# Two weight loads of a feed-forward stage issued by GpSimd, out of the queue of x's loads and stores

## The chip, the cores and the metric

One core of a Trainium2 chip runs the kernel. The metric is the device time of one execution in microseconds. The engines are named as the profile names them: PE is TensorE (matmuls), PEld its weight loads, DVE is VectorE, ACT is ScalarE, POOL is GpSimd, SP is SyncE; SPq and POOLq are the issues of transfers on SP and POOL.

## What is computed

One step of a hybrid encoder layer for a prompt of 512 frames and a sample of 64: adaLN modulation, an input projection, sparse attention, a Mamba-2 scan, a gated merge, and a SwiGLU feed-forward, all in float32. The change lies where the merge's output projection ends and the feed-forward begins:

```python
mixed = (g_attn * (o_attn @ w_branch_attn) + g_ssm * (y @ w_branch_ssm)) @ w_out
x = x + gt1 * mixed
h2 = rms_normalize(x) * g_norm_ffn * (1.0 + sc2) + sh2
gate, up = jnp.split(h2 @ w_gate_up, 2, axis=-1)
x = x + gt2 * ((jax.nn.silu(gate) * up) @ w_down)
```

D_MODEL is 1024, the feed-forward is 2816 wide; `gt1`, `sc2`, `sh2` and `gt2` are pieces of the adaLN modulation `silu(c) @ w_ada`.

## The kernel before

The kernel is written against a planner (`Plan`). Each operation is recorded, and `order` plays all of them through a model of costs, queues and latencies, and so fixes in which order each engine issues its instructions; `emit` then writes them out. Every instruction therefore has the line of the helper, L533, in the profile, and groups are told apart by the names of tiles. Since the order of an engine is fixed, an instruction that waits holds up all behind it on that engine. `R.after(ops)` adds edges to the planner's model alone; it makes no semaphore.

The 576 frames are held transposed, channels on partitions, in two halves of 288 columns (`hf` 0 and 1). A float32 product is made of three float32r matmuls, with both operands split in a high and a low part: `wh`, `wl` for weights, `mh`, `ml` for the merged activations, `xh…`, `xl…` for the feed-forward's input. ScalarE rounds the high part, VectorE subtracts to get the low one.

The output projection makes eight blocks `a` of 128 channels (`pwo0` to `pwo7`), 24 matmuls for each half. Blocks 0 to 4 are done both halves together; of blocks 5, 6 and 7 the first half comes first, then the second. Two PSUM slots named `mm` serve blocks 0 to 6 in turn, so block 6 takes the slot of block 4; block 7 lies in `px` and `py`. After each block and half, `residual` runs: VectorE adds `gt1 * mixed` to x in two pieces (256 and 32 columns, prompt and sample), ScalarE squares the result (`sq`) and scales it into `y2` (256 and 32 columns), VectorE adds the squares up (`sqa`). x is loaded from `x_d` by SyncE, in four buffers (`x2`, bufs=4): when a block is done, its x is stored, and the x of four blocks later is loaded into the same buffer. When the squares of block 7 are in, six small matmuls (`px<-ones,sqa`) sum them, GpSimd takes the power -1/2, TensorE spreads it over the partitions, and VectorE and ScalarE make the feed-forward's operands `xhA`, `xlA`.

In the same stretch `ada_columns(10, ...)` works out a piece of the modulation: GpSimd issues eight loads of `w_ada`, 256 KB each, into two buffers named T1 and T2 in turn (the trace leaves numbers out: `T<-in_w_ada`); VectorE multiplies each into two accumulators (T3, T4), which frees the buffer for the next but one, and two groups of eight small matmuls (`px<-T,pick`) end it.

The feed-forward's weights come in 22 slices `f`. `load_f(f)` loads two tiles of 512 KB, rows of 512 bytes, 128 x 8 of them: `g` (rows for the gate, tag `raw`, two buffers that the output projection's weights use too) and `u` (for the up part, tag `rawu`, two buffers of its own). `g0`, `u0` stand for those of slice 0, and so on; the third use of a `rawu` buffer, u2 and u3, waits until u0 and u1 are used up. `prepare` makes one operand out of a quarter of such a pair. Operands 6 and 7 are the two quarters of u1; they have buffers of their own (`wx`), so they can be made before the products start. The slices 0 and 1 are done plainly, the others by Strassen's scheme with seven products; all of them are bound to a list, `steps`, and TensorE walks through it.

SyncE's one queue carries, in this stretch, the last weights of the output projection, the loads and stores of x, and all the feed-forward's weights.

Of the kernel before, what the change touches and what calls it, by code (L numbers as in the profile page):

```python
# [13 lines left out]
P = 128  # L14
# [9 lines left out]
DFF = 2816  # L24
# [516 lines left out]
def build(tc, I, O):  # L541
    R = Plan(tc)
    vec, act, pool, pe, sync = R.vec, R.act, R.pool, R.pe, R.sync
# [51 lines left out]
    def kview(src2d):  # L595
        return src2d.rearrange("(k p) n -> p k n", p=P)
# [209 lines left out]
    x_d = R.dram([P, 8, 2, TH], F32, name="x_d")  # L806
# [762 lines left out]
    xqh, xql = {}, {}  # L1569
    ffw = R.mkpool("ffw", reuse_waits="tile")  # L1570
    x2p = R.mkpool("x2", reuse_waits="tile")
    x2 = {}

    y2 = {(j, hf): x2p.tile([P, 2, TW], F32, name=f"y2{j}{hf}") for j in range(4) for hf in range(2)}
    sqa = [x2p.tile([P, TH], F32, name=f"sqa{hf}") for hf in range(2)]

    def load_x2(a):
        x2[a] = x2p.tile([P, 2, TH], F32, name=f"x2{a}", tag="x2", bufs=4)
        sync.dma_start(x2[a], x_d[:, a])

    for a in range(4):
        load_x2(a)
# [6 lines left out]
    def residual(a, ps, hf, last):  # L1589
        x = x2[a][:, hf]  # L1590
        for s, c0, n in SEG:
            vec.scalar_tensor_tensor(x[:, c0:c0 + n], ps[:, c0:c0 + n], gt1h[:, a, s:s + 1], x[:, c0:c0 + n], op0=OP.mult, op1=OP.add)
        if a == 0:
            act.activation(sqa[hf], x, AF.Square)
        else:
            sq = x2p.tile([P, TH], F32, name=f"sq2{a}{hf}", tag="sq2", bufs=2)
            act.activation(sq, x, AF.Square)
            vec.tensor_tensor(sqa[hf], sqa[hf], sq, OP.add)
        for s, c0, n in SEG:
            act.activation(y2[a // 2, hf][:, a % 2, c0:c0 + n], x[:, c0:c0 + n], AF.Copy, scale=A2[:, a, s:s + 1])  # L1600
        if hf == 1:
            sync.dma_start(x2_d[:, a], x2[a])
            if a + 4 < 8:
                load_x2(a + 4)
# [81 lines left out]
    w_gu = I["w_gate_up"][0]  # L1686
# [4 lines left out]
    def load_f(f):  # L1691
        g = wp.tile([P, 8, P], F32, name=f"rawg{f}", tag="raw", bufs=2)
        u = ffw.tile([P, 8, P], F32, name=f"rawu{f}", tag="rawu", bufs=2)
        sync.dma_start(g, kview(w_gu[:, P * f:P * f + P]))
        sync.dma_start(u, kview(w_gu[:, DFF + P * f:DFF + P * f + P]))
        rawf[f] = {"B11": g[:, 0:4], "B21": g[:, 4:8], "B12": u[:, 0:4], "B22": u[:, 4:8]}

    def weight_sum(f, q):
# [10 lines left out]
    def prepare():  # L1709
        j = made[0]  # L1710
        f, q = preps[j]
        pl, tag, bufs = (x2p, "wx", 2) if 6 <= j < NP0 else (wp, ("wh", "wl")[j % 2], NWH)
        wops[f, q] = t = pl.tile([P, 8, P], F32R, name=f"wf{j}", tag=tag, bufs=bufs)
        src = rawf[f][q] if q[0] == "B" else weight_sum(f, q)
        act.activation(t[:, 0:4], src, AF.Copy)
        vec.tensor_tensor(t[:, 4:8], src, t[:, 0:4].bitcast(F32), OP.subtract)
        left[f] -= 1
        if left[f] == 0 and f + 2 < NFT:
            load_f(f + 2)
        made[0] += 1  # L1720
# [90 lines left out]
    def free_after(j):  # L1811

        return -1 if j < NP0 else N0 // 2 + j - NP0 if j < NP0 + 6 else N0 + j - 6 - NP0

    load_f(0)
    load_f(1)
    for i, (f, w, x, b, starts, *p) in enumerate(steps):
        if i in LATE_OPERANDS:
# [275 lines left out]
```

## Time and profile before

| | us |
|---|---|
| runs of the kernel (three) | 1373.69, 1377.72, 1378.02 |
| their median | 1377.72 |
| the profiled execution | 1373.19 |
| its span in the trace | 1371.4 |

Times in the trace count from the start of the span. A line of a timeline has the start, the length, the engine, the operation with `out<-in` and its shape, the number of instructions merged, and in brackets the idle time before it with what ended it. For a transfer the line is the issue on the queue's engine; its landing is told apart. A chain of waits is followed back from the last instruction: at each step to what released it.

### The profile page before, as it was taken

What the parts mean: (1) busy time and instruction counts of PE and PEld (TensorE: products, weight loads), DVE (VectorE), ACT (ScalarE), POOL (GpSimd) and SP (SyncE); (2) the same over time, 40 slices, a digit from 0 to 9 for tenths busy, and PEclk for the clock granted to TensorE, in tenths of its full rate; (3) what the DMA queues carried; (4) which work ended last, traced back from release to release, by engine and by line L of the source; (5) the groups of instructions that cost most, each with busy time, mean ns of one, the idle gap of its engine ahead of it and who ended that gap; (6) DMA issues with size and microseconds to landing.
All of it is one profiled execution on the core that took longest, in us unless ns stands there. A gap on an engine that the chain in (4) does not pass through costs nothing.

```text
span 1371.4 us, 27780 instructions
## 1 busy us (share of the span) xinstructions
PE 1351.2 (99%) x10705; PEld 1312.2 (96%) x10705; DVE 1112.1 (81%) x2249; ACT 735.4 (54%) x1535; POOL 248.7 (18%) x374
## 2 busy tenths in 40 slices
PE   7999999999999999999999999999999999999998
PEld 5899999999999999999999999999999999999998
DVE  4688999787778798888887688867899998878564
ACT  5445343677776666666665342224576666665221
POOL 1312002230310245545553200000000000000000
PEclk9999999999999999999999999999999999999999
DMA  9762335574754544444445598758233343325431
GB/s 286 235 173 88 106 105 152 130 187 101 178 140 115 175 127 122 136 130 139 132 122 163 180 319 262 241 164 241 91 93 98 104 137 94 93 72 160 121 107 36
DMA packets 269556, 200.70 MB, mean 146 GB/s; under 512 B 25200, under 2 KB 241424, under 8 KB 269424
## 3 DMA queue, kind: packets, MB, share of 16 engines
q1 hardware_dynamic: 265760, 185.82, 45.5%
q0 software_dynamic: 3664, 13.11, 4.7%
q8 instruction: 84, 1.38, 0.4%
q14 instruction: 48, 0.39, 0.1%
HBM read 158.33 MB, written 29.55 MB: 137 GB/s over the span
## 4 chain that ended last, share of the span: by engine, by line
PE 87%; DVE 5%; DMA 4%; ACT 2%; SPq 1%; issue 1%; ACTq 0%; DVEq 0%
PE mm L533 61%; PE py L533 15%; PE px L533 11%; DMA stage<-y_d 2%; DVE score L533 1%; DVE m L533 1%; DMA raw<-in_w_in 1%; SPq L533 1%; DVE wl L533 1%; DMA xt<-in_x_sample 1%; DMA rawu<-in_w_gate_up 0%; ACT wh L533 0%; ACT wl L533 0%; ACT qst L533 0%; DVE cu L533 0%
## 5 line engine op out<-in xcount | busy, mean ns | idle before, releaser
L533 ACT ACTIVATE wh<-raw 128x1024 fp32r<-128x1024 f32 (+3 forms) x152 | 148.9, 982 | 181.5 <-PE mm L533 128.3
L533 PE MATMUL mm<-hTh,wh 128*128 128x288 f32 (+1 forms) x1024 | 235.9, 306 | 0.6 <-ACT hTh L533 0.4
L533 PE MATMUL mm<-hTh,wl 128*128 128x288 f32 (+1 forms) x1024 | 232.0, 301 | 0.0
L533 PE MATMUL mm<-hTl,wh 128*128 128x288 f32 (+1 forms) x1024 | 230.1, 302 | 0.0
L533 PEld LDWEIGHTS mm<-hTh,wh 128*128 128x128 f32 (+1 forms) x1024 | 166.9, 189 | 4.0 <-issue 1.1
L533 PEld LDWEIGHTS mm<-hTh,wl 128*128 128x128 f32 (+1 forms) x1024 | 166.4, 188 | 2.7 <-issue 1.6
L533 PEld LDWEIGHTS mm<-hTl,wh 128*128 128x128 f32 (+1 forms) x1024 | 165.7, 189 | 2.4 <-issue 1.2
L533 DVE TENSOR_TENSOR wl<-raw,wh 128x1024 fp32r<-128x1024 f32 (+2 forms) x109 | 132.6, 1217 | 27.5 <-ACT wh L533 24.2
L533 DVE SCALAR_TENSOR_TENSOR cu<-xc,wc,cu 128x579 f32<-128x579 f32 x96 | 83.1, 865 | 2.1 <-ACT cu L533 1.5
L533 PE MATMUL mm<-wl,hTh 128*128 128x256 f32 x256 | 72.4, 284 | 0.0
L533 PE MATMUL mm<-wh,hTl 128*128 128x256 f32 x256 | 72.3, 284 | 0.0
L533 PE MATMUL mm<-wh,hTh 128*128 128x256 f32 x256 | 71.9, 284 | 0.0
L533 DVE SCALAR_TENSOR_TENSOR aacc<-adr,sil,aacc 128x512 f32<-128x512 f32 x84 | 60.2, 758 | 5.1 <-DMA adr<-in_w_ada 4.9
L533 PE MATMUL mm<-yh,wl 128*128 128x288 f32 x256 | 55.9, 297 | 0.0
L533 ACT ACTIVATE P<-lg,mn 128x128 f32<-128x128 f32 (+4 forms) x72 | 41.7, 581 | 25.4 <-DVE mn L533 24.2
L533 PE MATMUL mm<-yl,wh 128*128 128x288 f32 x256 | 54.8, 296 | 0.4 <-DVE yl L533 0.4
L533 PE MATMUL mm<-xhS,wh 128*128 128x290 f32 (+1 forms) x248 | 55.2, 297 | 0.0
L533 PE MATMUL mm<-yh,wh 128*128 128x288 f32 x256 | 54.9, 297 | 0.0
L533 PE MATMUL mm<-xhS,wl 128*128 128x290 f32 (+1 forms) x232 | 51.2, 296 | 0.0
L533 ACT ACTIVATE dec<-dec,nacs 128x128 f32<-128x128 f32 x128 | 42.5, 392 | 12.9 <-POOL dec L533 12.9
L533 PEld LDWEIGHTS mm<-wl,hTh 128*128 128x128 f32 x256 | 48.2, 189 | 0.4 <-issue 0.2
L533 PEld LDWEIGHTS mm<-wh,hTl 128*128 128x128 f32 x256 | 48.1, 189 | 0.3
(508 smaller groups left out, 3974.4 us busy)
## 6 DMA issues: line engine op xcount, KB each, us to landing
raw<-in_w_in SPq DMA_DIRECT2D x80, 512.0 KB, 3.9
adr<-in_w_ada SPq DMA_DIRECT2D x36, 512.0 KB, 5.6
rawu<-in_w_gate_up SPq DMA_DIRECT2D x22, 512.0 KB, 3.8
raw<-in_w_gate_up SPq DMA_DIRECT2D x22, 512.0 KB, 3.7
wl<-raw POOLq DMA_DIRECT2D x21, 512.0 KB, 4.9
bc<-acs_d SPq DMA_DIRECT2D x32, 256.0 KB, 3.4
raw<-in_w_branch_ssm SPq DMA_DIRECT2D x16, 512.0 KB, 4.6
raw<-in_w_down SPq DMA_DIRECT2D x16, 448.0 KB, 3.9
```

What stands on the lines that cost most here:

```text
L533: getattr(engines[x.eng], x.fn)(*[real(a) for a in x.args], **{k: real(v) for k, v in x.kw.items()})
```

## The change

The loads of u0 and u1 are issued by GpSimd; the loads of g0 and g1, and of all later slices, stay on SyncE. In the planner's model, u0 is put after the load of x of block 4 and u1 after that of block 5.

```diff
-    x2 = {}
+    x2, x2_load = {}, {}
...
     def load_x2(a):
         x2[a] = x2p.tile([P, 2, TH], F32, name=f"x2{a}", tag="x2", bufs=4)
-        sync.dma_start(x2[a], x_d[:, a])
+        x2_load[a] = sync.dma_start(x2[a], x_d[:, a])
...
         sync.dma_start(g, kview(w_gu[:, P * f:P * f + P]))
-        sync.dma_start(u, kview(w_gu[:, DFF + P * f:DFF + P * f + P]))
+        if f < 2:
+            with R.after([x2_load[4 + f]]):
+                pool.dma_start(u, kview(w_gu[:, DFF + P * f:DFF + P * f + P]))
+        else:
+            sync.dma_start(u, kview(w_gu[:, DFF + P * f:DFF + P * f + P]))
```

## The prediction

> **What bounds the kernel now.** I read the page first, for the engine that sets the end.
>
> ```profile
> span 1371.4 us, 27780 instructions
> ...
> PE 1351.2 (99%) x10705; PEld 1312.2 (96%) x10705; DVE 1112.1 (81%) x2249; ACT 735.4 (54%) x1535; POOL 248.7 (18%) x374
> ...
> PE 87%; DVE 5%; DMA 4%; ACT 2%; SPq 1%; issue 1%; ACTq 0%; DVEq 0%
> ```
>
> TensorE is busy 1351.2 of 1371.4 us and makes 87% of the chain that ended last. The change touches loads near 940 to 975 us, so the next view is the table by stretches, for that place and all of the gate-up stage behind it (columns: stretch, its length, then busy time of PE, PEld, DVE, ACT, POOL, the clock, DMA share, GB/s).
>
> ```profile
> 952.00:1000.00 48.00, 46.71 (x354) 45.05 (x354) 37.10 (x73) 27.95 (x60) 1.73 (x2) 1.00 0.37 108
> 1000.00:1225.00 225.00, 224.44 (x1684) 223.50 (x1683) 209.60 (x386) 143.68 (x285) 0.00 (x0) 1.00 0.34 101
> ```
>
> TensorE idles 48.00 - 46.71 = 1.29 us in the first and 225.00 - 224.44 = 0.56 us in the second, at full clock. With the same matmuls before and after, no better order of loads can gain more than 1.29 + 0.56 = 1.85 us there. The list of TensorE's waits from 900 us on names the pieces (total, times, longest):
>
> ```profile
> PE px L533 <- DVE sqa L533: 1.0, 1, 1.0
> ...
> PE py L533 <- DVE uu L533: 0.6, 1, 0.6
> ```
>
> The first has its history in the chain of waits (start, length, what):
>
> ```profile
> 952.68 6.27 DMA rawu<-in_w_gate_up
> ...
> 958.97 0.64 ACT wx L533
> ...
> 960.24 0.68 DVE wx L533
> ...
> 964.51 0.76 PE px L533 x6
> ```
>
> So u1, the second-half weights of slice 1, issued by SyncE at 952.68, lands at 958.95. ScalarE and VectorE make `wx` of it, and only then go on to the residual that stands behind `wx` in their order; its squares feed the six small matmuls at 964.51. The timeline of TensorE shows what the wait cost:
>
> ```profile
> 952.85 0.43 PE L533 MATMUL px<-T,pick 128*32 128x128 f32 x8
> ...
> 957.31 0.30 PE L533 MATMUL px<-ml,wh 128*128 128x288 f32 x1
> ...
> 960.24 0.30 PE L533 MATMUL px<-mh,wl 128*128 128x288 f32 x1
> ...
> ...
> 964.51 0.76 PE L533 MATMUL px<-ones,sqa 128*128 128x1 f32 x6 [1.04 <-DVE sqa L533]
> ...
> 972.53 0.30 PE L533 MATMUL mm<-xhA,wh 128*128 128x290 f32 x1
> ```
>
> While the other engines sat 4.35 us, TensorE worked on other products of w_out, one each 0.133 us (23 from 957.31 to 960.24), and lost only 1.04 us.
>
> **The change part by part.** What is removed are two of SyncE's issues, with what waited behind them; what is added are two issues on GpSimd. These are the rows of both queues:
>
> ```profile
> 946.40 0.51 SPq L533 DMA_DIRECT2D rawu<-in_w_gate_up  x1
> ...
> 952.68 0.53 SPq L533 DMA_DIRECT2D rawu<-in_w_gate_up  x1
> 953.30 1.37 SPq L533 DMA_DIRECT2D raw<-in_w_gate_up  x1
> ...
> 960.95 0.37 SPq L533 DMA_DIRECT2D rawu<-in_w_gate_up  x1
> ```
>
> ```profile
> 936.57 0.55 POOL L533 DMA_DIRECT2D T<-in_w_ada  x1 [0.78 <-DVE T L533]
> 942.16 0.55 POOL L533 DMA_DIRECT2D T<-in_w_ada  x1 [5.04 <-DVE T L533]
> 943.48 0.55 POOL L533 DMA_DIRECT2D T<-in_w_ada  x1 [0.78 <-DVE T L533]
> ```
>
> *Where they go.* In the built order of the changed program GpSimd issues T (936.57), u0, T (942.16), u1, T (943.48). `R.after` puts an edge in the planner only: in the built order u0 waits for an old transfer and u1 for none, so neither waits for a load of x. u0 starts at 936.57 + 0.55 = 937.1; u1 behind the next T, at 942.16 + 0.55 = 942.7, 10 us ahead of its issue before. SyncE saves 0.51 + 0.53 us of issue, which is on no path.
>
> *What the new issue costs* is not in this trace: GpSimd issues no transfer with 128 x 8 rows of 512 bytes here. The nearest rows, by tile (ns min/median/max of the issue, then us to landing), are its 256 KB loads with 128 rows and its 512 KB accumulating transfers with 128 rows:
>
> ```profile
> L533 POOL DMA_DIRECT2D T<-in_w_ada x8: 546/546/653, 913.2 to 943.5; - x8
> ...
> DMA to landing us min/median/max: 3.7/4.3/5.1
> ```
>
> ```profile
> L533 POOL DMA_DIRECT2D wl<-raw x21: 836/860/1194, 225.5 to 418.7; - x21
> ...
> DMA to landing us min/median/max: 4.5/4.9/7.5
> ```
>
> If an issue costs by instruction it takes 0.55 us; if wholly by row, 8 x 0.546 = 4.4 us; by the accumulating row 8 x 0.86 = 6.9 us. I take 4.4 us: T is the same kind of plain load from HBM, and a fixed part would only lower it. From the end of the issue to landing, 512 KB took 4.9 - 0.86 = 4.0 us. So u1 lands at 942.7 + 4.4 + 4.0 = 951.1 (bounds: 947.3 with 0.55 us; with 6.9 us u0's issue ends at 944.0 and holds up T and u1, 944.0 + 0.55 + 6.9 + 4.0 = 955.5).
>
> *When it is wanted.* The planner moves `wx` up on ScalarE and VectorE: in the built order it stands ahead of the last 32 columns of the residual of block 4, not behind that of block 5. These are the rows of VectorE and of ScalarE there:
>
> ```profile
> 946.68 2.74 DVE L533 SCALAR_TENSOR_TENSOR T<-T,sil,T 128x512 f32<-128x512 f32 x4 [0.26 <-DMA T<-in_w_ada]
> 949.76 0.64 DVE L533 SCALAR_TENSOR_TENSOR x<-mm,gt1h,x 128x256 f32<-128x256 f32 x2 [0.34 <-PE mm L533]
> 950.59 1.23 DVE L533 TENSOR_TENSOR wl<-raw,wh 128x1024 fp32r<-128x1024 f32 x1 [0.18 <-ACT wh L533]
> 951.73 0.45 DVE L533 TENSOR_TENSOR sqa<-sqa,sq 128x288 f32<-128x288 f32 x1
> ...
> 959.63 1.29 DVE L533 TENSOR_TENSOR wx<-rawu,wx 128x512 fp32r<-128x512 f32 x2 [4.36 <-ACT wx L533]
> 960.84 0.64 DVE L533 SCALAR_TENSOR_TENSOR x<-mm,gt1h,x 128x256 f32<-128x256 f32 x2
> ```
>
> ```profile
> 950.86 0.43 ACT L533 ACTIVATE sq<-x 128x288 f32<-128x288 f32 x1
> 951.20 0.31 ACT L533 ACTIVATE y<-x,A 128x32 f32<-128x32 f32 x1
> ...
> 958.97 1.15 ACT L533 ACTIVATE wx<-rawu 128x512 fp32r<-128x512 f32 x2 [4.35 <-DMA rawu<-in_w_gate_up]
> ...
> 971.92 0.62 ACT L533 ACTIVATE wh<-raw 128x512 fp32r<-128x512 f32 x1
> ```
>
> ScalarE ends its 32 columns at 951.5, scales 256 more of the second half (about 0.4) and is at `wx` at 951.9: that is the time by which u1 must have landed; 951.1 is 0.8 us ahead of it. Then ScalarE is done at 951.9 + 1.15 = 953.05; VectorE's second `wx` starts some 0.15 later and takes half of 1.29, to 953.85, and the last 32 columns take 0.24, to 954.1. These free the PSUM slot that the next w_out product (block 6) takes. TensorE meanwhile does what it has: to 952.85, and 10 products of block 7 that the new order puts there, 10 x 0.133, to 954.2. So the new wait is worth 0 to 0.2 us; I take 0.2. Queued behind it are VectorE's residuals and, through the slot, TensorE.
>
> *What is late next.* From 954.3 TensorE has 24 products of block 6 and 14 of block 7, and two groups of T matmuls at 0.43 each: 954.3 + 38 x 0.133 + 0.9 = 960.2. The residual of block 7 (0.64), ScalarE's squares (0.43) and VectorE's sum (0.45), with the steps between (0.2 each, as an estimate), give 962.3. TensorE is then in the products of the second half, 18 of which stand ahead of the sums: 960.2 + 2.4 = 962.6. The sums no longer wait, and the 1.04 us are gone. The gate-up stage, started at 972.53, starts 1.04 - 0.2 = 0.84 us earlier, and goes on at TensorE's pace.
>
> *The other moved steps* cost nothing, each by its cover. The last T goes out behind u1, at 942.7 + 4.4 = 947.1 and lands 4.3 later, at 951.4; VectorE wants it after the residual of block 5, near 954.8. Of the four T operations at 946.68 two are left there, so the T of 942.16 may land 949.76 - 946.68 - 1.4 = 1.7 us later than it does. SyncE's load of u3 (960.95) now stands ahead of g1 (953.30) and waits for `wx`, 953.9: g1 goes out some 1 us later, and its first reader is ScalarE at 971.92.
>
> **The sum.** The profiled execution took 1373.19 us, 1.8 over its span; -1.04 + 0.2 = -0.84 makes it 1372.35. The runs shown are 1373.69 to 1378.02, with their median at 1377.72, 4.5 us above the profiled one; the same -0.84 makes that 1376.9. A difference of about 0.3%, 4.1 us, is what a measurement of this kernel can tell from no change.
>
> [...] The stretches around the issues, with the DMA share in the last column but one:
>
> ```profile
> 936.00:946.00 10.00, 10.00 (x77) 10.00 (x77) 8.71 (x19) 5.86 (x14) 1.64 (x3) 1.00 0.88 270
> 946.00:952.00 6.00, 6.00 (x47) 6.00 (x47) 5.22 (x10) 2.10 (x5) 0.00 (x0) 1.00 0.66 198
> 952.00:958.00 6.00, 6.00 (x55) 5.29 (x55) 2.66 (x9) 2.00 (x6) 0.00 (x0) 1.00 0.92 242
> ```
>
> [...]
>
> The eight T issues took 546 to 653 ns, and VectorE was busy 8.71 of the 10 us in which three of them lie. [...]
>
> **The rivals.**
> 1. *u1 comes late, and slower.* The place is ScalarE's `wx`, now ahead of a PSUM slot that TensorE wants. It decides from a landing of 951.9 on; from there each us is a us on TensorE. With 6.9 us of issue: 955.5 - 951.9 + 0.2 - 1.04 = +2.7, 1380.4 us. With twice T's rate, 8.7 us, u1 lands at 937.1 + 8.7 + 0.55 + 8.7 + 4.0 = 959.1, which is +6.4, 1384.1 us. It passes 4.1 us at an issue of 7.6 us. For it speaks that 1024 rows of 512 bytes on this queue are shown nowhere and that two issues stand in a row before u1; against it, the 0.55 us.
> [...]
> 3. *All idle time goes,* -1.85: 1375.9. It needs the 0.6 us wait on `uu` to go too, which no moved instruction feeds.
>
> **How the numbers follow.** Forecast 0.50, rival 1 0.27, rival 2 0.15, rival 3 0.08. The predicted time is the forecast's, 1376.9. The lower end is the lowest run less the whole idle time, 1373.69 - 1.85 = 1371.8; the upper is rival 1 at twice T's rate, 1384.1; some 0.15 lie outside. Faster by over 0.3% would need more than TensorE's idle time: 0.03 for the spread of the runs. Of rival 1, 0.17 lie beyond 4.1 us. Within it stays 0.80.
>
> **What would show it.** Right: u1's issue near 942.7 on GpSimd, under 5 us long; ScalarE's `wx` near 952 with no wait on `rawu`; no wait of TensorE on `sqa`; the first gate-up product near 971.7. Wrong: GpSimd issues of 7 us or more, the T of 942.16 late, and a wait of TensorE on the residual `x` near 954 to 960. A gain above 1.85 us would mean that TensorE's busy time there hides waits, and my bound falls.

## The result, and the profile after

| | before | after |
|---|---|---|
| median of 22 runs each | 1375.33 us | 1372.35 us |
| lowest and highest | 1371.69 to 1380.73 | 1370.34 to 1375.45 |
| the profiled execution | 1373.19 | 1372.06 |
| its span | 1371.4 | 1370.4 |

The ratio is 0.9976, with a 95% interval of 0.9967 to 0.9985: a gain of about 3 us, or 0.24%. It is under the 0.3% that the prediction called the smallest difference that can be told, but with 22 runs on each side the interval lies clear of 1. The lowest runs differ by 1.35 us and the highest by 5.28: what went away are mostly the long executions.

The page of the changed kernel: TensorE is busy as long as before in a shorter span.

```profile
span 1370.4 us, 27779 instructions
...
PE 1351.5 (99%) x10705; PEld 1312.5 (96%) x10705; DVE 1112.8 (81%) x2249; ACT 735.8 (54%) x1535; POOL 250.8 (18%) x376
```

The table by stretches, with the columns of before's table (length, busy time of PE, PEld, DVE, ACT, POOL, clock, DMA share, GB/s):

```profile
936.00:946.00 10.00, 10.00 (x77) 10.00 (x76) 8.71 (x18) 5.22 (x12) 3.86 (x6) 1.00 1.00 313
946.00:952.00 6.00, 6.00 (x47) 6.00 (x46) 4.08 (x9) 2.60 (x7) 0.00 (x0) 1.00 0.74 245
952.00:958.00 6.00, 6.00 (x47) 6.00 (x46) 5.03 (x11) 3.19 (x9) 0.00 (x0) 1.00 0.72 189
952.00:1000.00 48.00, 48.00 (x366) 46.59 (x365) 39.51 (x77) 28.52 (x62) 1.75 (x2) 1.00 0.32 97
1000.00:1225.00 225.00, 224.77 (x1686) 223.83 (x1685) 209.09 (x385) 143.47 (x284) 0.00 (x0) 1.00 0.34 101
```

The 1.29 us in which TensorE idled between 952 and 1000 are gone. The transfers have moved: the DMA share of 936 to 946 went from 0.88 to 1.00, that of 952 to 958 from 0.92 to 0.72. GpSimd's timeline around u1, and below it what the rows of the tile `rawu` on GpSimd's queue say of its two issues and of their landing:

```profile
942.58 0.55 POOL L533 DMA_DIRECT2D T<-in_w_ada  x1 [3.92 <-DVE T L533]
943.12 0.90 POOL L533 DMA_DIRECT2D rawu<-in_w_gate_up  x1
944.01 0.55 POOL L533 DMA_DIRECT2D T<-in_w_ada  x1
```

```profile
L533 POOL DMA_DIRECT2D rawu<-in_w_gate_up x2: 899/906/913, 937.7 to 943.1; - x2
...
DMA to landing us min/median/max: 5.9/6.0/6.0
```

An issue of 1024 rows of 512 bytes took 0.91 us, and u1 was there some 6.0 us after 943.12, at 949.1. ScalarE reached it later, and found nothing to wait for; VectorE followed; and the sums on TensorE have no wait ahead of them either (timelines of ScalarE, VectorE and TensorE):

```profile
952.44 1.14 ACT L533 ACTIVATE wx<-rawu 128x512 fp32r<-128x512 f32 x2
```

```profile
953.09 1.29 DVE L533 TENSOR_TENSOR wx<-rawu,wx 128x512 fp32r<-128x512 f32 x2 [0.16 <-ACT wx L533]
```

```profile
963.38 0.65 PE L533 MATMUL px<-ones,sqa 128*128 128x1 f32 x6
...
971.83 0.30 PE L533 MATMUL mm<-xhA,wh 128*128 128x290 f32 x1
```

Of TensorE's waits from 900 us on only two are left, both in later work:

```profile
PE px L533 <- DVE x2r L533: 0.7, 1, 0.7
PE py L533 <- DVE uu L533: 0.2, 1, 0.2
```

So the place and the mechanism are those foretold. The size isn't: the two traces differ by 1.0 us of span, the medians by 3.0. Times of two executions can't be set side by side directly either, since they have drifted apart before this stage begins. I therefore measure the stage by itself: from SyncE's first load of x's blocks to its ninth load of gate weights (`raw<-in_w_gate_up`), both of which stand on SyncE in every kernel. First and last row, of the kernel before and of the one after:

```profile
920.93 1.48 SPq L533 DMA_DIRECT2D x<-x_d  x3
...
1045.46 0.37 SPq L533 DMA_DIRECT2D raw<-in_w_gate_up  x1
```

```profile
921.57 1.48 SPq L533 DMA_DIRECT2D x<-x_d  x3
...
1044.20 0.37 SPq L533 DMA_DIRECT2D raw<-in_w_gate_up  x1
```

That is 1045.46 - 920.93 = 124.5 us before and 1044.20 - 921.57 = 122.6 after: 1.9 us are gained in the stage, and 0.6 of it is hidden in the spans by a later start. That is still 1.1 us short of the 3.0 between the medians; the last experiments look for them.

### The profile page after: what moved, and what is told of

It reads as the page before. It is cut to its first block, busy times and chain, and to the rows that moved or that the text cites. A ratio compares the mean times of both kernels' runs of the same rounds, so it can differ in the third digit from the quotient of the medians.

```text
span 1370.4 us, 27779 instructions
## 1 busy us (share of the span) xinstructions
PE 1351.5 (99%) x10705; PEld 1312.5 (96%) x10705; DVE 1112.8 (81%) x2249; ACT 735.8 (54%) x1535; POOL 250.8 (18%) x376
## 4 chain that ended last, share of the span: by engine, by line
PE 86%; DVE 7%; DMA 4%; ACT 2%; issue 1%; SPq 1%; ACTq 0%; DVEq 0%
PE mm L533 61%; PE py L533 14%; PE px L533 11%; DMA stage<-y_d 2%; DVE score L533 1%; DMA raw<-in_w_in 1%; DVE m L533 1%; DVE wl L533 1%; SPq L533 1%; DMA xt<-in_x_sample 1%; DVE y L533 0%; ACT wh L533 0%; DVE xlS L533 0%; DMA rawu<-in_w_gate_up 0%; ACT wl L533 0%
```

## The experiments

Theory A is that of the prediction: u1 lands after ScalarE wants it, all the rest follows from ScalarE's and VectorE's fixed order, and the cure is to part the landing from the want, by whatever means. Theory B: what counts is that SyncE's one queue is relieved, by whichever load leaves it. Theory C: what counts is the new order that the planner makes of the other engines' work. The diffs of u1 alone, u0 alone and both cures are against the changed kernel, the others against the kernel before; all times are compared with the kernel before. The first four ran beside 34 runs of it (median 1376.5), the next three beside 29 (1375.31).

### u1 alone, u0 alone

The kernel with u1 alone; in the one with u0 alone the condition is `f == 0`.

```diff
-        if f < 2:
+        if f == 1:
             with R.after([x2_load[4 + f]]):
                 pool.dma_start(u, ...)
```

> Only u1 is issued by GpSimd; u0 stays on SyncE. Theory A (what costs is that u1 lands late at wx, in-order on ScalarE and VectorE): the whole gain of the change is here, a ratio near 0.998 to before, no wait of wx on rawu, no wait of TensorE on sqa. Theory B (SyncE's queue is relieved of two loads, so x's loads and stores run earlier, whichever load leaves): about half the gain, near 0.999. Theory C (the planner's other order of the T operations and of block 7's products brings it): this order is near the changed kernel's too, so C expects the gain here as well.

> Only u0 is issued by GpSimd; u1 stays on SyncE, behind the store and the load of x of block 7 and g0. Theory A: u1 is issued near 952 as before and lands near 957 to 959, wx waits for it some 4 us, most of the gain is missing: ratio 0.9990 to 1.0005. Theory B: half the gain, near 0.999, with x's loads landing earlier. Theory C: the T operations and block 7's products are reordered much as in the changed kernel, so the gain is here, near 0.998.

u1 alone: 1372.63 us, ratio 0.9966 [0.9953, 0.9980]. u0 alone: 1375.60, ratio 0.9990 [0.9977, 1.0003]. ScalarE's rows, u1 alone first:

```profile
952.46 1.14 ACT L533 ACTIVATE wx<-rawu 128x512 fp32r<-128x512 f32 x2
```

```profile
959.96 1.15 ACT L533 ACTIVATE wx<-rawu 128x512 fp32r<-128x512 f32 x2 [4.17 <-DMA rawu<-in_w_gate_up]
```

Moving u1 gives all that the change gives, which is more than theory B allows for one load (0.999 lies outside the interval). Moving u0 leaves ScalarE's wait at 4.17 us, with nothing that can be told from no change. Its ratio by itself doesn't separate the theories: 0.9990 is what B expected and lies within what A expected. The loads of x of the last two blocks, which B wanted earlier, went out 26.3 and 30.4 us after the first load of x, against 25.1 and 30.9 before: one later, one a little earlier. In that kernel TensorE's wait shows at another operand, a copy that stands behind `wx` on VectorE:

```profile
PE py L533 <- DVE ra L533: 2.1, 1, 2.1
```

### u1 far earlier, on SyncE

```diff
-        sync.dma_start(u, ...)
+        with R.prio(9000 if f == 1 else R.offset):
+            sync.dma_start(u, ...)
```

> No load on GpSimd: u1 stays on SyncE, but at the head of its queue, ahead of the first load of x (near 920), and wx is made near 926. Theory A: the time of the issue counts, not the queue: no wait of wx, ratio near 0.998, unless x of block 0 or the weights of w_out, which now stand behind u1, come late and cost TensorE up to 1 us. Theory B (the other queue is what helps): SyncE's queue carries the same transfers as before, so ratio near 1.000.

1377.21 us, ratio 1.0002 [0.9990, 1.0014]. u1 went out at 920.47, the wait near 959 is gone, and another took its place 25 us earlier (SyncE, VectorE, TensorE):

```profile
920.47 0.53 SPq L533 DMA_DIRECT2D rawu<-in_w_gate_up  x1
921.06 1.51 SPq L533 DMA_DIRECT2D x<-x_d  x1
925.83 0.37 SPq L533 DMA_DIRECT2D raw<-in_w_out  x1
926.25 1.05 SPq L533 DMA_DIRECT2D x<-x_d  x2
```

```profile
927.84 1.28 DVE L533 TENSOR_TENSOR wx<-rawu,wx 128x512 fp32r<-128x512 f32 x2
...
932.12 0.64 DVE L533 SCALAR_TENSOR_TENSOR x<-mm,gt1h,x 128x256 f32<-128x256 f32 x2
```

```profile
932.81 0.53 PE L533 MATMUL mm<-mh,wh 128*128 128x288 f32 x2 [2.74 <-DVE x L533]
```

Before, three blocks of x went out together at 920.93; here two of them stand behind u1 and a load of w_out, to 926.25. `wx`, made at 927.84, stands ahead of residuals that free the PSUM slots, and TensorE loses 2.74 us. The earlier load was no gain in itself; it mattered what it was put in front of. Since the planner changed several things at once, I don't say which part of the 2.74 belongs to which.

### All transfers as before, only `wx` later

```diff
-            act.activation(y2[...], x[...], AF.Copy, scale=...)
+            scaled[a, hf] = act.activation(y2[...], x[...], AF.Copy, scale=...)
...
-        act.activation(t[:, 0:4], src, AF.Copy)
+        with R.after([scaled[7, 0]] if 6 <= j < NP0 else []):
+            act.activation(t[:, 0:4], src, AF.Copy)
```

> All transfers stay as before, u0 and u1 on SyncE in the same order, and TensorE's order is the same; only the wx operations stand behind the residual of block 7's first half on ScalarE and VectorE, so that nothing of the sums' chain waits behind u1. Theory A: the gain is here without any transfer moved: ratio near 0.998, u1 lands at the same 958 to 959, TensorE has no wait on sqa. Theory B: ratio near 1.000, since the queue is as full as before. Theory C: near 1.000 too, since TensorE's order is as before.

1373.56 us, ratio 0.9975 [0.9962, 0.9987]. SyncE issues u1 no earlier than before, and ScalarE comes to it only when block 7's first half is done:

```profile
954.69 0.53 SPq L533 DMA_DIRECT2D rawu<-in_w_gate_up  x1
```

```profile
963.72 0.43 ACT L533 ACTIVATE sq<-x 128x288 f32<-128x288 f32 x1
964.27 1.14 ACT L533 ACTIVATE wx<-rawu 128x512 fp32r<-128x512 f32 x2
```

This is the whole gain without a second issuer, which speaks against B. In the built program TensorE, GpSimd and SyncE have the order of before, instruction by instruction, and on ScalarE and VectorE only the two `wx` instructions have moved; that speaks against C.

### One instruction moved in SyncE's queue, ahead and behind

Here the planner's order is kept for every engine, and only the one issue of u1 is moved in the finished sequence: two of SyncE's transfers ahead in one kernel (the diff), two behind in the other (`move_u1(2)`). Ahead, it passes the load of x of block 7 and g0; behind, g1 and a store of x. In the built programs all other instructions stand where they did.

```diff
     def run(self):
         self.order()
+        self.move_u1(-2)
```

> The kernel before with one instruction moved: SyncE issues the second half of slice 1's weights (u1) before, not after, the load of x's block that it waits with; the next weight load is passed too. Every other engine's instructions and their order are as before, and SyncE stays the only issuer. Theory A (u1 lands after ScalarE wants it, and only that costs): u1 is issued at about 947.5 us instead of 952.7, lands about 6 us later at 953.5 to 954.0, ScalarE waits under 1 us for it instead of 4, TensorE's stall on the sum of squares' operands goes, and the time is that of the kernel with u1 on GpSimd, a ratio of 0.996 to 0.998. Rival B (one queue carries too much, so a second issuer is what pays): ratio 0.999 to 1.001, the queue having as much in it as before. Rival D (x's block, now issued 0.5 us later, is as urgent): its first reader waits and the ratio is 1.000 or above.

> The kernel before with one instruction moved the other way: u1 behind the next weight load and the store of x after it, every other engine's order as before. Theory A with a price of one to one: u1 is issued 2.4 to 4.6 us later (955.1 to 957.3 us), ScalarE's wait grows from about 4.2 to 6.6 to 8.8 us and TensorE's idle time in 950 to 1000 grows by as much; time 2.4 to 4.6 us above the kernel before, a ratio of 1.0017 to 1.0034. Rival (the late load costs only what the profile of before showed, 1.04 us, the rest being hidden): ratio 1.000 to 1.001.

Ahead: 1373.47 us, ratio 0.9980 [0.9967, 0.9994]. Behind: 1379.99, ratio 1.0029 [1.0016, 1.0041]. SyncE and ScalarE of the kernel with u1 ahead:

```profile
949.25 0.38 SPq L533 DMA_DIRECT2D rawu<-in_w_gate_up  x1
953.69 0.32 SPq L533 DMA_DIRECT2D x<-x_d  x1
```

```profile
956.82 1.14 ACT L533 ACTIVATE wx<-rawu 128x512 fp32r<-128x512 f32 x2
```

and of the one with u1 behind, with TensorE's wait:

```profile
958.25 0.43 SPq L533 DMA_DIRECT2D rawu<-in_w_gate_up  x1
```

```profile
965.60 1.15 ACT L533 ACTIVATE wx<-rawu 128x512 fp32r<-128x512 f32 x2 [6.54 <-DMA rawu<-in_w_gate_up]
```

```profile
PE px L533 <- DVE sqa L533: 3.2, 1, 3.2
```

In the first, u1 leaves 4.4 us before the load of x that waits for its buffer, on the same queue, and the gain is there, though u1 went out at 949.25 and not at the expected 947.5. This settles it against B and C: nothing but u1's place behind a waiting load has changed. In the second ScalarE's wait grew by 2.2 us (6.54 against 4.35) and TensorE's by 2.2 (3.2 against 1.0), one to one as expected. The 4.7 us between the medians are more than that; a lower clock, told below, goes with it. What is left of the queue's relief can't be told here; the intervals of the kernel ahead in SyncE's queue and of the changed kernel overlap.

### Both cures at once

```diff
-        if f < 2:
+        if f == 1:
...
+        with R.after([scaled[7, 0]] if 6 <= j < NP0 else []):
```

> Both cures at once: u1 issued by GpSimd, and the two weight preparations that read it placed behind the first half of block 7's residual on ScalarE and VectorE. The planner also moves the last two accumulations of the modulation on VectorE. Theory A: each cure alone takes the whole stall away, so together they give no more than either: a ratio of 0.996 to 0.998, TensorE idle in 950 to 1000 under 0.5 us. Rival (each takes a part of the loss): the two add up, ratio 0.994 to 0.9955.

1372.60 us, ratio 0.9977 [0.9966, 0.9989]. The gains of the two cures don't add up: once the wait is gone, nothing is left to take. No version that I ran is below the changed kernel by more than the intervals allow.

### The same kernels, profiled again

The unchanged kernel before was profiled four more times, the changed one once more.

> The kernel before, profiled a second time. If u1's landing moves from execution to execution, then SyncE's issue of it or its landing differs from 952.68 and 958.95 us by over 0.5 us, and ScalarE's wait and TensorE's stall on it move by the same amount. If it doesn't, all three are within 0.3 us of the first profile, and the spread of the kernel before (1371.8 to 1382.8 us) has another source.

> The kernel before, profiled a third time. The stage is measured from SyncE's first load of x's blocks (the first of x, at about 921 us) to its ninth load of gate weights (at about 1046 us): 124.6 us in the first profile, 123.2 in the second, 122.7 in the changed kernel. Theory (u1's lateness changes from execution to execution, and both profiles of before so far were lucky): this stage is longer than 123.2 us again, ScalarE's wait for u1 over 3 us, and the execution's time above 1373.2 us goes with a longer stage, by one to one once the drift up to 921 us is taken off. Rival (the spread comes from before 921 us only): the stage is 123.2 to 124.6 us whatever the time.

> The kernel before, a fourth time, as for the third: theory, the stage from the first load of x to the ninth load of gate weights takes 124 to 128 us; rival, 123.2 to 124.6 us.

> The kernel before, a fifth time, as for the third: theory, the stage from the first load of x to the ninth load of gate weights takes 124 to 128 us; rival, 123.2 to 124.6 us.

> The changed kernel profiled a second time. Theory: u1 lands some 3 us before it is wanted, so the stage from the first load of x to the ninth load of gate weights is within 0.5 us of the first profile's 122.7 us, and TensorE idles under 0.5 us in 950 to 1000. Rival: it varies as in the kernel before, by 1 us and more.

ScalarE's row for `wx` in the second, third, fourth and fifth profile of the kernel before:

```profile
959.17 1.15 ACT L533 ACTIVATE wx<-rawu 128x512 fp32r<-128x512 f32 x2 [3.20 <-DMA rawu<-in_w_gate_up]
```

```profile
962.22 1.15 ACT L533 ACTIVATE wx<-rawu 128x512 fp32r<-128x512 f32 x2 [7.04 <-DMA rawu<-in_w_gate_up]
```

```profile
959.59 1.16 ACT L533 ACTIVATE wx<-rawu 128x512 fp32r<-128x512 f32 x2 [4.96 <-DMA rawu<-in_w_gate_up]
```

```profile
960.25 1.15 ACT L533 ACTIVATE wx<-rawu 128x512 fp32r<-128x512 f32 x2 [4.86 <-DMA rawu<-in_w_gate_up]
```

TensorE's wait on `sqa` in the third and the fourth:

```profile
PE px L533 <- DVE sqa L533: 3.8, 1, 3.8
```

```profile
PE px L533 <- DVE sqa L533: 1.6, 1, 1.6
```

Side by side, with the stage as above (first load of x to ninth load of gate weights) and the clock of 950 to 1000:

| execution | time | ScalarE waits for u1 | TensorE waits on `sqa` | clock | stage |
|---|---|---|---|---|---|
| before, second | 1373.10 | 3.20 | 0 | 1.00 | 123.1 |
| before, first | 1373.19 | 4.35 | 1.0 | 1.00 | 124.5 |
| before, fifth | 1374.13 | 4.86 | 1.5 | 1.00 | 124.9 |
| before, fourth | 1373.51 | 4.96 | 1.6 | 1.00 | 124.9 |
| before, third | 1378.51 | 7.04 | 3.8 | 0.93 | 129.7 |
| after, first | 1372.06 | 0 | 0 | 1.00 | 122.6 |
| after, second | 1371.90 | 0 | 0 | 1.00 | 123.1 |

Two things are to be seen. First, TensorE has some 3.3 us of other work beside the wait: 4.35 - 1.0, 4.86 - 1.5, 4.96 - 1.6 and 7.04 - 3.8 are all 3.2 to 3.4, and so is 6.54 - 3.2 in the kernel with u1 behind. In the second profile the 3.20 us are hidden whole, and the kernel before loses nothing. From there, in these executions, each us of lateness was a us on TensorE.

Second, the third profile lost more than its wait: against the first, 2.8 us more of wait, but 5.2 us more of stage. The other 2.4 us go with the clock. TensorE's timeline there:

```profile
963.61 0.29 PE L533 MATMUL mm<-mh,wh 128*128 128x288 f32 x1
967.75 1.21 PE L533 MATMUL px<-ones,sqa 128*128 128x1 f32 x6 [3.85 <-DVE sqa L533]
968.89 0.61 PE L533 MATMUL mm<-ml,wh 128*128 128x288 f32 x1
969.29 0.44 PE L533 MATMUL mm<-mh,wl 128*128 128x288 f32 x1
969.53 0.44 PE L533 MATMUL mm<-mh,wh 128*128 128x288 f32 x1
```

After the wait the products come every 0.24 us instead of every 0.133. The table by stretches of the same execution, with the columns of the tables above, shows the clock in the last column but two; below it is a stretch of the kernel with u0 alone:

```profile
968.00:972.00 4.00, 4.00 (x19) 3.97 (x20) 2.42 (x7) 1.51 (x4) 0.88 (x1) 0.50 0.17 67
972.00:974.00 2.00, 2.00 (x12) 1.79 (x12) 0.22 (x1) 0.00 (x0) 0.00 (x0) 0.76 0.59 163
```

```profile
964.00:966.00 2.00, 2.00 (x11) 2.00 (x10) 0.81 (x3) 1.11 (x4) 0.00 (x0) 0.51 0.56 167
```

TensorE is busy all the time there, at half the clock. In stretches of a quarter of a us the clock of the third profile was 0.50 from 966.1 to 972.9 us, that is from the middle of the wait on for 6.8 us. It was 0.50 for 3.4 us in the kernel with u1 behind (972.9 to 976.3, after a wait of 3.2 us that ended at 971.14) and in the one with u0 alone (964.1 to 967.5, after one of 2.1 us that ended at 962.54). After the 2.74 us in the kernel with u1 far earlier it stayed at 1.00, and so it did around the `sqa` waits of 1.6 us or less. So a single wait of 2.1 us was followed by a clock of 0.50, while one of 2.74 us was not. What decides between these two was not tried.

The lower clock goes with the lateness over many runs too. Over the 63 runs of the kernel before that stood beside the experiments, the mean granted clock of the span was 0.997 or lower in 22, with a median of 1378.68 us, and higher in 41, with one of 1375.11. It was that low in 9 of the 12 runs with u1 behind, in 1 of the 22 runs of the changed kernel, and in 4 of the 47 runs of the four other kernels without the wait.

So theory A holds: the lateness of u1 is a quantity with a spread, ScalarE's wait being 3.2 to 7.0 us in five executions, and in both executions of the changed kernel the wait is gone. The stage's mean is 125.4 us in the five profiles of before and 122.9 in the two of after; they differ by 2.6 us before rounding, and the mean times of these executions, 1374.49 and 1371.98, by 2.5. That is near the 3.0 us of the medians, but it hangs on the third profile: without it both differences are 1.5 us. So where the gain comes from is shown, and how its 3.0 us divide between wait and clock is only estimated.

The other kernels bear out the place. The stage took 122.7 to 123.2 us in the one profile of each of the four without the wait (u1 alone, `wx` later, u1 ahead in the queue, both cures), 127.8 with u1 behind and 127.4 with u0 alone. The expectation that the kernel before keeps a stage of 123.2 to 124.6 us whatever its time is refuted by the third profile, with 129.7; that the changed kernel varies by 1 us and more did not show, with 0.5 us between its two profiles. Part of the spread comes from elsewhere all the same: over all kernels of this study whose order is alike up to there, the first load of x went out between 920.9 and 925.4 us.

Why u1's lateness varies was not tried. Both of its parts do: SyncE issued it between 952.33 and 954.78 us, behind a load that waits for a buffer, and ScalarE started 5.8 to 7.4 us after that.

## Why the prediction was right, and where it was not

*The place and the chain* were right: u1, `wx` in its fixed place, the residual and the squares behind it, TensorE's sums. u1 alone on GpSimd, `wx` alone later, and u1 two places ahead in its queue each take the loss away.

*Where they go.* Right: u1 behind the T at 942.58, at 943.12 (foretold 942.7), waiting for no load of x.

*What the new issue costs.* The value I took, 4.4 us by counting rows against T, was far off: 0.90 us, near the lower bound of 0.55. Eight times as many rows with twice the bytes cost 0.36 us more than T; the accumulating transfers of the same 512 KB in 128 rows had taken 0.86. The landing after the issue's end was off the other way: 6.0 - 0.9 = 5.1 us instead of 4.0, in a stretch with a DMA share of 1.00. Together, u1 at 949.1 instead of 951.1.

*When it is wanted:* 952.44, foretold 951.9; the slack is 3.3 us, not 0.8. *The new wait* is 0, not 0.2.

*What is late next.* Right: nothing. The first gate-up product comes at 971.83 (foretold 971.7), though by a stage that began 0.6 us later. The covers held: VectorE takes the last two T's at 955.0 and 956.4 with no wait, and u3 goes out ahead of g1, 2.2 us later than g1 did before, without a trace on TensorE:

```profile
954.45 0.38 SPq L533 DMA_DIRECT2D rawu<-in_w_gate_up  x1
...
955.51 0.43 SPq L533 DMA_DIRECT2D raw<-in_w_gate_up  x1
```

*The sum* was mis-sized: -0.84 us forecast, about -3.0 measured. The step that failed is the first one, that no order of loads can gain more than the 1.85 us of idle time that the trace shows, and with it the term of -1.04 us. Both hold for the one execution that was profiled. The wait behind the term was 0 in the second profile, and 3.8 us in the third, with some 2.4 us more lost at the lower clock: it is an average that was wanted, and one sample was put in its place. Idle time was no bound where the clock fell, for TensorE at half the clock counts as busy (in the third profile 4.00 of the 4.00 us from 968 to 972, at 0.50); the prediction had said that a gain above 1.85 us would mean that TensorE's busy time hides waits, and what it hides, in executions other than the profiled one, is the lower clock. The sign was there to be read: the profiled execution lay 4.5 us below the median of the runs, and I noted that and then applied the same term to the median. The predicted 1376.9 us also stood on a median of three runs, 1377.72, that 22 runs put at 1375.33. That the measured 1372.35 lies in the stated range, 0.5 us above its lower end, is luck: that end is the lowest of three runs less the 1.85 us that don't bound the gain.

*The rivals.* u1 late and slower: this did not come; that a later u1 costs time was right (the kernel with u1 behind shows it, +4.7 us between medians), the issue's price was not. No gain (rival 2): this is refuted, since the gain comes from the place in the queue, and the kernel with u1 two places ahead on SyncE alone has it without a second issuer. All idle time goes: the idle time of 952 to 1000 did go; the wait on `uu` was 0.2 us in one profile of after and 0.7 in the other, so its change from 0.6 meant nothing. None of the forecast and the rivals had a gain as large as 3.0 us.

*The chances.* I gave 0.80 to a difference within 0.3%, and 0.24% came; the 0.03 for more was little for a term with such a spread.

## What to carry to other kernels

Here a load that ScalarE waited for in order cost TensorE the part of the wait that TensorE's remaining work didn't cover: nothing of a wait of 3.20 us, and 1.0, 1.5, 1.6 and 3.8 us of waits of 4.35, 4.86, 4.96 and 7.04. So measure this cover (here some 3.3 us of products on TensorE) and the spread of the wait over several profiles. The gain of the cure, as an estimate from these profiles, was the mean of the excess and of what went with the lower clock (some 2.4 us in the third profile), not the stall of 1.0 us that the first profile showed. When the profiled execution lies well below the median of the runs, ask first which wait is longer in the others. Before a second issuer is tried, look whether the late load stands behind a waiting one in its queue: two places ahead (ratio 0.9980), or the reader put later (0.9975), did the same here as the second issuer (0.9976).

## What was not expected of the hardware

- GpSimd's issue of 512 KB in 1024 rows of 512 bytes took 0.90 us, where 256 KB in 128 rows took 0.55 and an accumulating transfer of 512 KB in 128 rows 0.86: hardly a price by the row.
- TensorE waits of 2.1, 3.2 and 3.8 us went with a clock of 0.50 for 3.4, 3.4 and 6.8 us; one of 2.74 us and those of 1.6 us or less did not. In the third profile this took some 2.4 us on top of the wait.
